# One run of probability-value products per head pair, in a two-layer hybrid trunk

## Chip, cores and metric

The kernel runs on one core of a Trainium2 chip. The metric is device time of one execution in microseconds (us). TensorE runs matmuls (PE in the profile, its weight loads PEld), VectorE is DVE, ScalarE is ACT, GpSimd is POOL, and SyncE (SP) issues most transfers.

## What is computed

Two layers over 2048 latent tokens and 256 context tokens of width 1024. Each layer norms and modulates the tokens, projects them to four head groups (a gated linear recurrence, a Fourier mix, a banded window attention, a two-dimensional neighbourhood attention), gates each group, projects back and adds to the stream. The change touches only the last step of both attentions, probabilities times values:

```python
p = jax.nn.softmax(jnp.concatenate([s_loc, s_ctx, sink_l], axis=-1), axis=-1).astype(v.dtype)
nw = 3 * SWA_BLOCK
o = (jnp.einsum('bkgnqj,bknjd->bkgnqd', p[..., :nw], v_win)
     + jnp.einsum('bkgnqc,bkcd->bkgnqd', p[..., nw:nw + CTX_LEN], vcx))
...
p = jax.nn.softmax(jnp.concatenate([s_nb, s_ctx], axis=-1), axis=-1).astype(v.dtype)
o = (jnp.einsum('bhrqkw,bhrkwd->bhrqd', p_nb, v_rows)
     + jnp.einsum('bhrqc,bhcd->bhrqd', p[..., kh * GRID_W:], vcx))
```

## The kernel before, in words

Attention works on items: one head and 128 queries. `attend` (L830) multiplies keys and queries into the one score buffer of PSUM (`pse`), DVE adds the bias and finds the row limit (L836), ACT takes the exponential (L844) into `S`. `transpose_p` turns `S` by chunks of 128 keys (L862, output `ppt`, two buffers), and the turned chunks are copied to SBUF as `pt`: the first three of a head in one copy by DVE (L872), the remaining ones in one copy by ACT (L870). For the second head of a pair it also turns the reciprocal row sums (L866) and ACT copies them (`rt`, L868). `head_out` multiplies: for each chunk `c` and each of the two heads `x` of a pair one product (L921), 128 keys by 64 value columns against 128 queries, at array position column 0 for the first head and column 64 for the second, all summed in one PSUM buffer `py`. DVE scales the result (L924). A pair has 4, 8, 10 or 12 products, and there are 136 pairs in the two layers: 1360 products, each of which the trace records as two passes. In the traced names `vd` are values of latent tokens and `vc` values of context tokens, which are the last two chunks.

`pipeline` issues the parts of neighbouring items in turn, so that the products of a pair come three items after its scores. Between these items stand the projections, `mm3` (L220 to L222, outputs `ps` of the input projections and `pso` of the output projection): three products for each 128 of 1024, on the whole 128x128 array. They are independent of the attention around them, and are called the filler below.

Nobody writes the order of an engine's queue by hand. A scheduler places the instructions of the whole program by priority (program order, unless `high_priority` raises it) and by when its model thinks that inputs and buffers are there; each engine then executes its queue in that order, and waits where something is late. Weights, activations of `prep_h` and `reload_h`, and values come by DMAs from SP.

```python
for c in range(n):
    for x, h in enumerate((r[6], r)):
        nc.tensor.matmul(py[64 * x:64 * x + 64, 0:128], h[2][c], h[5][0][c], ...)
```

`r` is the pair's second head, `r[6]` its first, `h[2]` the value chunks, `h[5][0]` the copied chunks `pt`.

Of the kernel before, what the change touches and what calls it, by code (L numbers as in the profile page):

```python
# [37 lines left out]
class Kern:  # L38
# [865 lines left out]
    def head_out(self, pool, st, i, r, stage, out):  # L904

        nc = self.nc
        S, rc, vs = r[0:3]
        if stage == 0:
            r.append(self.transpose_p(pool, S, len(vs), rc if i else None))
            if i == 0:  # L910
                st["first"] = r
            r.append(st["first"])
            return
        if i == 0:
            return
        if stage == 1:
            py = st["py"] = self.py.tile([128, 512], F32, tag="y", name="py")
            n = len(vs)
            for c in range(n):
                for x, h in enumerate((r[6], r)):  # L920
                    nc.tensor.matmul(py[64 * x:64 * x + 64, 0:128], h[2][c], h[5][0][c], start=(c == 0), stop=(c == n - 1), tile_position=(0, 64 * x))  # L921
            return
        c = out.shape[-1]
        nc.vector.tensor_tensor(out=out, in0=st["py"][:, 0:128].rearrange("p (r c) -> p r c", c=c), in1=r[5][1].rearrange("p (r c) -> p r c", c=c), op=ALU.mult)  # L924
# [457 lines left out]
```

## Time and profile before

| | |
|---|---|
| median of 3 runs | 3062.85 us (3062.26 to 3063.51) |
| the profiled execution, its own time | 3059.56 us |
| span of that execution | 3057.7 us |
| PE busy in the span | 93% (PEld 80%) |
| DVE, ACT, POOL busy | 53%, 35%, 27% |
| granted TensorE clock, mean | 0.959 |
| HBM traffic over the span | 149 GB/s |

A matmul's end in the trace is modelled, its start is recorded, so what a matmul costs in a stream of them is read from the start of one to the start of the next. A line of the timeline merges neighbours of one kind: "x3" are three passes, the time is from the first start to the last end. The last of them starts its own duration (0.27 us for `py` and `ppt`) before that end.

### The profile page before, as it was taken

The page shows a single profiled execution, that of the slowest core. Times are in us where ns is not written, and L with a number is a line of the kernel's source. Part 1 is how long each engine was busy: PE and PEld are TensorE (multiplying, and loading weights), DVE is VectorE, ACT ScalarE, POOL GpSimd, SP SyncE. Part 2 cuts the span into 40 slices and gives each one's busy share as a digit, 9 for nine tenths or more (in the row PEclk, how much of TensorE's full clock was granted, in tenths as well). Part 3 has the DMA queues.
Part 4 walks back from the last instruction along what each step waited for, and adds up shares of the span by engine and source line. Part 5 has one row for each costly group of instructions (what it writes and reads, how often), then busy time and mean ns, then how long its engine had stood idle before and what let it go on. Part 6 is the DMA issues. An engine that isn't in the chain of part 4 may idle for free. (4 is left out here: it accounts for less than half of the span.)

```text
span 3057.7 us, 56121 instructions
## 1 busy us (share of the span) xinstructions
PE 2854.0 (93%) x21206; PEld 2447.1 (80%) x21206; DVE 1618.5 (53%) x3741; ACT 1073.4 (35%) x2344; POOL 836.8 (27%) x922
## 2 busy tenths in 40 slices
PE   5989979978999999999979989999889999999998
PEld 5879879967777777777879889899778777777788
DVE  7554864475455444545654553465564546455453
ACT  3333323322343332434224323343223444343332
POOL 3242322343222111311132432333342213111132
PEclk9989979989999999999989899899999999999999
DMA  8634634254654263542554664242546643446365
GB/s 265 196 110 149 190 110 128 91 175 145 179 155 136 83 189 109 166 133 92 191 159 148 195 183 142 87 132 89 165 148 188 175 130 110 148 127 187 110 189 188
DMA packets 476684, 458.05 MB, mean 150 GB/s; under 512 B 54763, under 2 KB 355565, under 8 KB 476013
## 3 DMA queue, kind: packets, MB, share of 16 engines
q1 hardware_dynamic: 472782, 440.66, 47.2%
q0 software_dynamic: 3616, 13.64, 1.9%
q8 instruction: 173, 2.83, 0.4%
q14 instruction: 113, 0.93, 0.1%
HBM read 339.56 MB, written 114.60 MB: 149 GB/s over the span
## 5 line engine op out<-in xcount | busy, mean ns | idle before, releaser
L220 PE MATMUL ps<-whi,hh 128*128 128x256 f32 x1968 | 587.3, 298 | 33.6 <-ACT hh L258 18.2
L222 PE MATMUL ps<-whi,hl 128*128 128x256 f32 x1968 | 584.2, 297 | 9.1 <-DVE hl L259 9.1
L221 PE MATMUL ps<-wlo,hh 128*128 128x256 f32 x1968 | 583.1, 296 | 6.8 <-PEq L639 6.8
L213 POOL TENSOR_TENSOR wlo<-wraw,whi 128x512 fp32r<-128x512 f32 x208 | 284.7, 1369 | 831.3 <-ACT whi L212 801.9
L220 PEld LDWEIGHTS ps<-whi,hh 128*128 128x128 f32 x1968 | 393.0, 200 | 46.9 <-ACT hh L258 20.1
L220 PE MATMUL ps<-hh,whi 128*128 128x256 f32 x1376 | 405.6, 295 | 5.9 <-DVE nsq L376 2.6
L222 PEld LDWEIGHTS ps<-whi,hl 128*128 128x128 f32 x1968 | 391.9, 199 | 21.8 <-DVE hl L259 12.9
L221 PE MATMUL ps<-hl,whi 128*128 128x256 f32 x1376 | 405.9, 295 | 0.0
L221 PEld LDWEIGHTS ps<-wlo,hh 128*128 128x128 f32 x1968 | 393.0, 200 | 15.1 <-issue 12.8
L222 PE MATMUL ps<-hh,wlo 128*128 128x256 f32 x1376 | 404.5, 294 | 0.0
L844 ACT ACTIVATE S<-S,am 128x641 f32<-128x641 f32 (+5 forms) x272 | 226.0, 831 | 502.7 <-DVE am L836 490.3
L212 ACT CAST whi<-wraw 128x512 fp32r<-128x512 f32 x416 | 242.9, 620 | 428.1 <-DMA wraw<-w_in 193.4
L220 PE MATMUL pso<-mh,whi 128*128 128x256 f32 x1088 | 320.4, 295 | 7.3 <-DVE xo L1106 5.0
L222 PE MATMUL pso<-mh,wlo 128*128 128x256 f32 x1088 | 319.0, 294 | 3.0 <-POOL wlo L213 1.9
L221 PE MATMUL pso<-ml,whi 128*128 128x256 f32 x1088 | 318.4, 293 | 0.0
L221 PEld LDWEIGHTS ps<-hl,whi 128*128 128x128 f32 x1376 | 264.8, 192 | 35.8 <-issue 35.5
L220 PEld LDWEIGHTS ps<-hh,whi 128*128 128x128 f32 x1376 | 264.7, 192 | 32.2 <-issue 24.3
L222 PEld LDWEIGHTS ps<-hh,wlo 128*128 128x128 f32 x1376 | 264.4, 192 | 26.9 <-issue 26.5
L213 DVE TENSOR_TENSOR wlo<-wraw,whi 128x512 fp32r<-128x512 f32 x208 | 192.9, 931 | 170.4 <-ACT whi L212 162.2
L191 POOL TENSOR_TENSOR rs<-ms,mhalf 128x8 f32<-128x8 f32 (+2 forms) x140 | 172.1, 1231 | 314.6 <-DVE ms L189 305.6
L830 PE MATMUL pse<-kst,q 64*128 64x256 f32 (+2 forms) x1184 | 243.8, 457 | 3.2 <-DVE am L836 2.3
L220 PEld LDWEIGHTS pso<-mh,whi 128*128 128x128 f32 x1088 | 213.0, 196 | 25.4 <-issue 19.5
(203 smaller groups left out, 5052.8 us busy)
## 6 DMA issues: line engine op xcount, KB each, us to landing
wraw<-w_in SPq DMA_DIRECT2D x288, 256.0 KB
wraw<-w_out SPq DMA_DIRECT2D x128, 256.0 KB
adaw<-ada_w SPq DMA_DIRECT2D x82, 256.0 KB
scr_g<-ev SPq DMA_DIRECT2D x68, 256.0 KB
g<-scr_g SPq DMA_DIRECT2D x34, 512.0 KB
y<-scr_y SPq DMA_DIRECT2D x34, 512.0 KB
bias<-nbias SPq DMA_DIRECT2D x48, 256.0 KB
scr_h<-x SPq DMA_DIRECT2D x22, 512.0 KB
```

Of the source, the lines that this page charges most:

```text
L191: nc.gpsimd.tensor_tensor(out=rs, in0=ms, in1=self.mhalf.to_broadcast([128, n]), op=ALU.pow)
L212: nc.scalar.copy(hi[:, k], raw)
L213: (nc.gpsimd if i % 4 else nc.vector).tensor_tensor(out=lo[:, k], in0=raw, in1=hi[:, k], op=ALU.subtract)
L220: nc.tensor.matmul(out, ah(k), bh(k), start=(k == 0), stop=False)
L221: nc.tensor.matmul(out, ah(k), bl(k), start=False, stop=False)
L222: nc.tensor.matmul(out, al(k), bh(k), start=False, stop=(k == KB - 1))
L830: nc.tensor.matmul(p[:, lo:hi], q[r], k, start=True, stop=True, tile_position=(64 * o, 0))
L844: nc.scalar.activation(out=S[:, 0:w], in_=S[:, 0:w], func=AF.Exp, scale=-1.0, bias=m[:, 0:1], accum_out=m[:, 1:2])
```

## The change

The products of a pair are issued under the scheduler's highest priority, from the last chunk to the first, and in each chunk the second head before the first. The first product of the run then reads a chunk that is copied last.

```diff
             py = st["py"] = self.py.tile([128, 512], F32, tag="y", name="py")
             n = len(vs)
-            for c in range(n):
-                for x, h in enumerate((r[6], r)):
-                    nc.tensor.matmul(py[64 * x:64 * x + 64, 0:128], h[2][c], h[5][0][c], start=(c == 0), stop=(c == n - 1), tile_position=(0, 64 * x))
+            with self.tc.high_priority():
+                for c in range(n - 1, -1, -1):
+                    for x, h in ((1, r), (0, r[6])):
+                        nc.tensor.matmul(py[64 * x:64 * x + 64, 0:128], h[2][c], h[5][0][c], start=(c == n - 1), stop=(c == 0), tile_position=(0, 64 * x))
```

How it moves TensorE's queue is shown for one pair of twelve products in the neighbourhood attention of layer 1, where the output projection is the filler. Before, the pair's products stand in three places. The first and second, with four filler products and the turning of another head's chunks between them:

```order
L921 MATMUL py<-pt,vd 64x128
L221 MATMUL pso<-ml,whi 128x256
L222 MATMUL pso<-mh,wlo 128x256
L220 MATMUL pso<-mh,whi 128x256
L862 MATMUL ppt<-idn,S 128x128 x3
L921 MATMUL py<-pt,vd 64x128 x6
```

One product stood alone, and six followed three filler products and three transposes later. The pair's last five come behind another head's transposes, which the scores of a third head split:

```order
L862 MATMUL ppt<-idn,S 128x128
L830 MATMUL pse<-kst,q 128x384
L830 MATMUL pse<-kst,q 128x128
L830 MATMUL pse<-kst,q 128x256
L862 MATMUL ppt<-idn,S 128x128 x2
L921 MATMUL py<-pt,vd 64x128
L921 MATMUL py<-pt,vc 64x128 x4
L862 MATMUL ppt<-idn,S 128x128 x3
```

The same pair with the change, on the same engine:

```order
L220 MATMUL pso<-mh,whi 128x256
L221 MATMUL pso<-ml,whi 128x256
L922 MATMUL py<-pt,vc 64x128 x4
L922 MATMUL py<-pt,vd 64x128 x8
L862 MATMUL ppt<-idn,S 128x128 x3
L830 MATMUL pse<-kst,q 128x384
L830 MATMUL pse<-kst,q 128x128
L830 MATMUL pse<-kst,q 128x256
L862 MATMUL ppt<-idn,S 128x128 x3
```

All twelve now stand together, context chunks first, behind filler, and the transposes of each later head stand together too. Over the whole queue the 1360 products stand in 456 places before and in 136 with the change, one for each pair. (L922 is L921 of before, one line further down.)

## Rows read from the trace of the kernel before

**Rows 1.** The page's head.

```profile
span 3057.7 us, 56121 instructions
```

**Rows 2.** Busy time in the two stages of attention: stretch, length, engines, clock, DMA.

```profile
780.00:1480.00 700.00, 690.72 (x5227) 529.46 (x5226) 347.86 (x823) 269.39 (x625) 144.30 (x229) 0.99 0.46 136
2315.00:2950.00 635.00, 632.78 (x4887) 485.47 (x4886) 327.16 (x749) 256.51 (x583) 142.05 (x218) 1.00 0.52 151
```

**Rows 3.** Groups by line and shape: count, busy us, mean ns, idle before, its cause.

```profile
L921 PE MATMUL py<-pt,vd 128*64 128x128 f32 x1632 | 208.6, 293 | 4.3 <-DVE yt L924 4.3
...
L872 DVE COPY pt<-ppt 128x384 f32<-128x384 f32 x256 | 142.1, 555 | 50.3 <-PE ppt L862 46.6
...
L921 PE MATMUL py<-pt,vc 128*64 128x128 f32 x1088 | 116.5, 279 | 0.7 <-DVE pt L872 0.7
...
L870 ACT COPY pt<-ppt 128x256 f32<-128x256 f32 x176 | 65.2, 370 | 28.4 <-PE ppt L862 27.1
...
L273 DVE TENSOR_TENSOR hl<-x,hh 128x1024 fp32r<-128x1024 f32 x11 | 14.2, 1286 | 8.4 <-ACT hh L272 8.4
```

**Rows 4.** TensorE's waits, 780 to 1480 us: us in total, times, longest.

```profile
PE py L921 <- DVE pt L872: 0.7, 1, 0.7
```

**Rows 5.** TensorE's timeline, last three of a ten-product pair's four places (start, duration).

```profile
2334.99 0.29 PE L222 MATMUL ps<-hh,wlo 128*128 128x256 f32 x1
2335.21 0.43 PE L921 MATMUL py<-pt,vd 128*64 128x128 f32 x2
2335.57 0.55 PE L862 MATMUL ppt<-idn,S 128*128 128x128 f32 x3
2336.05 0.43 PE L921 MATMUL py<-pt,vd 128*64 128x128 f32 x2
2336.41 0.44 PE L862 MATMUL ppt<-idn,S 128*128 128x128 f32 x2
2336.78 0.54 PE L921 MATMUL py<-pt,vd 128*64 128x128 f32 x5
...
2337.16 0.70 PE L921 MATMUL py<-pt,vc 128*64 128x128 f32 x7
2337.80 0.39 PE L220 MATMUL ps<-hh,whi 128*128 128x256 f32 x1
2338.02 0.28 PE L221 MATMUL ps<-hl,whi 128*128 128x256 f32 x1
2338.13 0.28 PE L222 MATMUL ps<-hh,wlo 128*128 128x256 f32 x1
```

**Rows 6.** TensorE's timeline, one transpose within filler.

```profile
2400.57 0.28 PE L221 MATMUL ps<-wlo,hh 128*128 128x256 f32 x1
2400.69 0.27 PE L866 MATMUL ppt<-idn,rd 128*128 128x128 f32 x1
2400.72 0.36 PE L222 MATMUL ps<-whi,hl 128*128 128x256 f32 x1
2400.91 0.28 PE L220 MATMUL ps<-whi,hh 128*128 128x256 f32 x1
```

**Rows 7.** TensorE's timeline, scores and transposes within filler, then products.

```profile
2406.83 0.28 PE L222 MATMUL ps<-whi,hl 128*128 128x256 f32 x1
2407.04 0.93 PE L830 MATMUL pse<-kst,q 64*128 64x384 f32 x6
2407.90 0.38 PE L220 MATMUL ps<-whi,hh 128*128 128x256 f32 x1
...
2408.60 0.49 PE L862 MATMUL ppt<-idn,S 128*128 128x128 f32 x3
2409.02 0.43 PE L921 MATMUL py<-pt,vd 128*64 128x128 f32 x2
```

**Rows 8.** TensorE's timeline, a pair whose ten products stand together already.

```profile
872.48 0.88 PE L921 MATMUL py<-pt,vd 128*64 128x128 f32 x12
873.19 0.60 PE L921 MATMUL py<-pt,vc 128*64 128x128 f32 x8
```

## Prediction

> **What bounds the kernel now.** I read busy time by stage first. The page gives a span of 3057.7 us [rows 1]; the two stretches that hold attention take 700 and 635 us of it [rows 2]. [...] DVE is busy 675 us of the same 1335, ACT 526, and the DMA engines half of the time. [...] The filler is independent work that fills every hole, so in these stretches whatever TensorE no longer has to issue comes off the end.
>
> A busy TensorE is not one that multiplies at its rate, so the second view is its timeline, start to start. The reader should see there that a change of matmul shape costs. Filler to filler is 0.12 us (2338.02 to 2338.13 and so on) [rows 5]. From filler to products it is 0.22 (2334.99 to 2335.21), from products to filler 0.21, taken as 0.20, and the step behind is again 0.22 instead of 0.12 [rows 5]. Transposes start 0.11 apart: three of them last 0.49 us, the last one 0.27, so its start lies 0.22 behind the first. From 2408.60 that leaves 0.42 - 0.22 = 0.20 to the product at 2409.02 [rows 7]. Behind products the same three transposes last 0.55 [rows 5] and not 0.49 [rows 7], so their second step is 0.06 slower. A single product holds 0.16 between its two passes (0.43 - 0.27) and 0.20 more to the transposes (2335.21 to 2335.57) [rows 5].
>
> **The change, part by part.** No product, load or copy is added or removed; the order of queues changes. The priced part is TensorE's. I counted neighbours in both orders, at the level of passes, and price the difference with the steps above.
>
> *Inside the runs.* Start of the first pass to start of the last is 0.16 us for one product [rows 5], 0.81 for seven (2336.78 to 2337.16 + 0.70 - 0.27 = 2337.59) [rows 5], 1.04 for ten (872.48 to 873.19 + 0.60 - 0.27 = 873.52) [rows 8]. So each further two products add 0.22, and an odd one costs as much as a pair. Before there are 275 runs of one or two, 54 of three or four, 80 of five or six, 32 of seven or eight, 14 of nine or ten and one of eleven: 275 x 0.165 + 54 x 0.38 + 80 x 0.60 + 32 x 0.82 + 14 x 1.04 + 1.26 = 155.4 us. Now there are 8 runs of four, 8 of eight, 88 of ten and 32 of twelve (1.26, one step beyond the longest row): 3.0 + 6.6 + 91.5 + 40.3 = 141.4. Gain 14.0.
>
> *Into and out of the runs.* Transposes to products fall from 315 to 6: 309 x 0.20 = 61.8 less. Products to filler fall from 220 to 5, each with its slower next step: 215 x 0.30 = 64.5 less. Products to transposes fall from 223 to 107: 116 x 0.26 = 30.2 less. Filler to products rises from 98 to 119: 4.6 more. Products to scores rises from 7 to 24, taken like filler to scores (2406.83 to 2407.04, 0.21) [rows 7]: 3.6 more. Together 148.3 less.
>
> *What closes the gaps.* The neighbours of a vanished run now touch. Transpose to filler rises from 217 to 405; it takes 0.03 us, and the step behind it 0.19 instead of 0.12 (2400.69, 2400.72, 2400.91) [rows 6], so 188 x 0.10 = 18.8 more. Filler to filler 121 x 0.12 = 14.5 more, transpose to transpose 57 x 0.11 = 6.3 more. Filler to transpose falls by 70: 8.4 less. Filler to scores falls by 75 and transpose to scores rises by 63: 2.5 less at 0.21 each. Scores are left for transposes 135 times more and for filler and products 131 times less; I take leaving them (0.86 us from their first start to the filler) [rows 7] as equally long whatever follows, so zero. Together 28.7 more.
>
> Sum: 14.0 + 148.3 - 28.7 = 133.6 us less on TensorE, about 1 us for each of 136 pairs.
>
> *The wait that it adds.* TensorE takes its queue in order. The first product of a run waits for the pair's last copy, and behind it stand filler and the next transposes, which formerly ran while a copy was late. In the pair shown above, 17 filler products, a group of scores and three transposes stand between the last transposes it needs and its run: about 3.6 us by the steps above. The copy takes 0.37 us on ACT or 0.56 on DVE, behind at most one long instruction, as the 1.29 us subtraction of `hl` [rows 3]; that is under 2 us. So most runs should start without a wait. Nearest rows for both ends: 0.7 us for all of a stretch [rows 4], and twice the present idle time, 23 us, when everything beside TensorE is a tenth tighter. I take 8, nearer the first, since the slack is over 1.5 us.
>
> *What becomes tighter.* DVE and ACT do the same work in 134 us less: DVE rises from 51% to 56% of the two stretches (675 of 1201). `py` is held for 1 us and not for a chain of runs, which only helps the next pair. DMA traffic rises in rate by a tenth from a half-full state [rows 2]. Each at nothing; the cover is the filler, and were it gone the copies would show as TensorE's waits.
>
> [...] DVE has 675 us of work in 1335 [rows 2], which leaves it room. [...]
>
> The sum against the profiled execution: 3059.6 - 133.6 + 8 = 2934.0. The median of the runs is 3.3 above that execution, so **2937 us**.
>
> **Rivals.**
>
> 1. *The copies wait in part.* The faster queue meets copies that DVE or ACT make behind other work, and the price is half of the gain: 3063 - 67 = 2996, between 2967 and 3057. For it: half of the chunks wait for one ACT instruction behind `rt`, and an in-order TensorE has no way round. Against it: the 3.6 us of cover above.
>
> 2. *The end runs over: slower.* At each of 136 runs TensorE stops for the last copy while the filler queues behind. At 134 / 136, about 1.0 us, of wait for each run the gain is gone; at 1.5 us it is 204 - 134 = 70 us slower, 3133. The copy would have to land 4.6 us and more behind its transposes. Against it: rows 3 and 4.
>
> 3. *Nothing is gained.* Something else was the bound, and the shape changes lay in its shadow: 3063, within 6. The candidate is the emptying of PSUM by DVE and ACT. It would show as TensorE waiting for DVE or ACT, and rows 2 and 4 show hardly any. [...]
>
> That the change does not do what it says is excluded by the order: one unbroken run for each pair.
>
> **How the numbers follow.** The forecast has 0.74. Its own range comes from the unknown terms: with no new wait, and 10 us for steps read to 0.01 us of which some 1000 changed, 3063 - 144 = 2919; with 23 us of waits and no gain inside the runs, 3063 - 120 + 23 = 2966. Rival 1 has 0.14, rival 2 0.06, rival 3 0.06. I set the range at 2915 to 2985: it takes the forecast's range and the nearer part of rival 1, and leaves out the rest of it and rivals 2 and 3. A measurement of this kernel tells about 0.2% (6 us) from no change. Faster by more than that: forecast and rival 1, 0.88. Within it: rival 3, 0.06. Slower: 0.06.
>
> **What would show it.** Right: 2720 passes of products in 136 runs of 0.4 to 1.3 us; the two stretches shorter by about 70 and 63 us (72 and 64 pairs at 1 us); TensorE's idle time in them under 25 us; the clock still 1.00 there; DVE's share near 56%. Wrong: product lines with several tens of us of idle time released by `pt` copies (rivals 1 and 2), TensorE waiting for score limits or exponentials (rival 1 or 3), a second step behind a shape change that moved to the scores, or stretches that kept their length.

## The result and the profile after

The change takes 2951.29 us (median of 4 runs, 2951.03 to 2952.43) against 3063.18 us before (4 runs, 3062.26 to 3065.11): 0.9635 of the time, 95% interval 0.9618 to 0.9651. It is faster by 112 us, inside the range of 2915 to 2985 and 14 us above the predicted 2937. The same kernel, run again beside later experiments, took 2953.8.

The head of the page after, which answers to [rows 1]:

```profile
span 2949.1 us, 55777 instructions
...
PE 2718.3 (92%) x21206; PEld 2410.2 (82%) x21206; DVE 1609.3 (55%) x3741; ACT 1070.9 (36%) x2344; POOL 837.3 (28%) x922
```

The span is 108.6 us shorter, and TensorE executes the same 21206 passes. For a fair comparison I cut both traces at the first and the last score matmul of each attention. The windows view of the kernel before, cut so (stretch, length, busy time of PE, PEld, DVE, ACT and POOL, TensorE's clock, DMA share, GB/s):

```profile
772.30:1470.10 697.80, 688.52 (x5199) 527.94 (x5198) 346.58 (x821) 269.62 (x625) 142.91 (x228) 0.99 0.47 138
1470.10:2320.50 850.40, 771.22 (x5662) 723.94 (x5658) 443.69 (x986) 269.35 (x560) 274.16 (x239) 0.93 0.48 149
2320.50:2930.30 609.80, 608.40 (x4680) 463.34 (x4681) 316.77 (x731) 250.68 (x570) 135.25 (x209) 1.00 0.51 149
```

The same view of the kernel after:

```profile
772.80:1433.80 661.00, 644.68 (x5430) 537.56 (x5431) 348.81 (x834) 273.33 (x630) 150.38 (x231) 0.99 0.51 151
1433.80:2264.10 830.30, 735.70 (x5430) 687.55 (x5426) 438.67 (x972) 264.88 (x555) 270.14 (x236) 0.93 0.48 148
2264.10:2833.90 569.80, 560.90 (x4785) 461.69 (x4786) 315.65 (x740) 251.68 (x575) 139.57 (x212) 0.99 0.57 167
```

The first and third lines are the two attentions, the second is the part between them (recurrences, Fourier mix, projections). Two things stand in the attentions. They are 36.8 and 40.0 us shorter, and TensorE executes 231 and 105 more passes in them than before: filler that formerly ran outside. Counted in the trace, the filler passes inside rose by 241 and 112. At 0.12 us each [rows 5] that is 28.9 and 13.4 us of other work taken along. The middle part and the end lose exactly this filler, and become shorter by somewhat less than it is worth: the middle by 20.1 us, where 241 passes are 28.9.

The group lines by shape (count, busy us, mean ns, idle before and its cause), which answer to [rows 3]:

```profile
L862 PE MATMUL ppt<-idn,S 128*128 128x128 f32 x1360 | 243.6, 284 | 10.4 <-DVE pt L872 5.2 <-ACT pt L870 3.9 <-ACT S L844 0.7
L830 PE MATMUL pse<-kst,q 64*128 64x384 f32 x480 | 219.6, 538 | 13.6 <-DVE am L836 12.5 <-DMA kst<-scr_kd 0.8 <-issue 0.2
...
L872 DVE COPY pt<-ppt 128x384 f32<-128x384 f32 x256 | 141.3, 552 | 18.1 <-PE ppt L862 17.3
L922 PE MATMUL py<-pt,vd 128*64 128x128 f32 x1632 | 110.8, 273 | 0.0
...
L922 PE MATMUL py<-pt,vc 128*64 128x128 f32 x1088 | 89.4, 285 | 0.0
```

The products (L922) keep TensorE busy for 200.2 us instead of 325.1, with no idle time before them, 5.0 before the change. The copies are as long as they were. What is new is idle time before the scores (L830), 13.6 us, nearly all released by DVE's row limit `am`, and before the transposes (L862), 10.4 us, released by the copies that empty `ppt`. Before the change it was 3.2 and about 0.6.

TensorE's timeline after, one pair of twelve products (start, duration):

```profile
2399.77 0.66 PE L922 MATMUL py<-pt,vc 128*64 128x128 f32 x8
2400.26 1.04 PE L922 MATMUL py<-pt,vd 128*64 128x128 f32 x16
2401.23 0.55 PE L862 MATMUL ppt<-idn,S 128*128 128x128 f32 x3
2401.71 0.93 PE L830 MATMUL pse<-kst,q 64*128 64x384 f32 x6
```

First pass to last pass is 2400.26 + 1.04 - 0.27 - 2399.77 = 1.26 us, as the prediction had it one step beyond its longest row. The step to the transposes is 0.20.

Where the new waits come from is in two views of one place. DVE's timeline after:

```profile
1049.92 1.23 DVE L1083 TENSOR_TENSOR y<-y,g 128x1024 f32<-128x1024 f32 x1 [4.32 <-DMA y<-scr_y]
1051.06 0.68 DVE L213 TENSOR_TENSOR wlo<-wraw,whi 128x512 fp32r<-128x512 f32 x1
1051.66 0.28 DVE L925 TENSOR_TENSOR yt<-py,rt 128x128 f32<-128x128 f32 x1
1051.86 0.68 DVE L213 TENSOR_TENSOR wlo<-wraw,whi 128x512 fp32r<-128x512 f32 x1
1052.46 0.55 DVE L872 COPY pt<-ppt 128x384 f32<-128x384 f32 x1
```

And TensorE's at the same moment:

```profile
1050.24 0.28 PE L221 MATMUL ps<-hl,whi 128*128 128x256 f32 x1
1053.07 0.90 PE L862 MATMUL ppt<-idn,S 128*128 128x128 f32 x3 [2.55 <-DVE pt L872]
1053.62 0.56 PE L222 MATMUL ps<-hh,wlo 128*128 128x256 f32 x1
1053.98 0.41 PE L220 MATMUL ps<-hh,whi 128*128 128x256 f32 x1
1054.19 0.41 PE L221 MATMUL ps<-hl,whi 128*128 128x256 f32 x1
```

L1083 belongs to `prep_mix`: it loads the mixed heads `y` and their gates `g` for 128 tokens, DVE multiplies them (L1083), ACT rounds the product (L1084), DVE or POOL subtracts (L1085), and the output projection reads it. DVE stands 4.32 us for the load of `y`, then multiplies, then does three short things, and only then the copy that TensorE has wanted since about 1050.5. The wait of TensorE is named after `pt`, but its cause is the load. All eleven waits of over 1 us before scores and transposes in the two attentions end 0.9 to 1.9 us behind an L1083 that had itself stood for 2.3 to 5.1 us, ten of them by name for its load (for the eleventh the trace names no releaser).

### The profile page after: what moved, and what is told of

It reads as the page before. It is cut to its first block, busy times and chain, and to the rows that moved or that the text cites. A ratio compares the mean times of both kernels' runs of the same rounds, so it can differ in the third digit from the quotient of the medians.

```text
span 2949.1 us, 55777 instructions
## 1 busy us (share of the span) xinstructions
PE 2718.3 (92%) x21206; PEld 2410.2 (82%) x21206; DVE 1609.3 (55%) x3741; ACT 1070.9 (36%) x2344; POOL 837.3 (28%) x922
## 2 busy tenths in 40 slices
DMA packets 476681, 458.00 MB, mean 155 GB/s; under 512 B 54763, under 2 KB 355565, under 8 KB 476013
## 5 line engine op out<-in xcount | busy, mean ns | idle before, releaser
L830 PE MATMUL pse<-kst,q 64*128 64x256 f32 (+2 forms) x1184 | 246.6, 457 | 13.6 <-DVE am L836 12.5
L862 PE MATMUL ppt<-idn,S 128*128 128x128 f32 x1360 | 243.6, 284 | 10.4 <-DVE pt L872 5.2
```

Of the source, the lines that this page charges most:

```text
L830: nc.tensor.matmul(p[:, lo:hi], q[r], k, start=True, stop=True, tile_position=(64 * o, 0))
L862: nc.tensor.transpose(p[:, i], S[:, (c0 + i) * 128:(c0 + i + 1) * 128], self.idn)
```

## The experiments

Times are medians. The ratio to the kernel before, run beside it on the same chip, stands with its interval. Kernels that did not run side by side are better compared by their ratios than by their times: TensorE's instructions ahead of the first attention are the same ones in the same order in eleven of the fourteen traces below, and this part takes 764 to 777 us in them. The filler moves between the parts of the program, so I compare lengths by one formula. Both attentions together take 1307.6 us before, with 4514 filler passes and 11.5 us of TensorE idle. Idle time counts the gap that ends at a stretch's first score too, so it is up to 2.3 us more than length less busy time. "Gain without waits" is what an attention got shorter, plus 0.12 us for each further filler pass in it, plus its further idle time. The price applies the median start-to-start step of each kind of neighbour in the trace before, told apart by what stands ahead of it too, to every neighbour in the new queue. This finer list gives 142 us for the change, where the prediction's list by hand gave 134. A price depends on the list: one that takes each run of products whole, by its length, gives 57 us for the priority alone, 114 for the order alone and 147 for the change, so I read the column as good to some 12 us.

| kernel | runs of products | time, us | priced gain | both attentions, us | filler passes | idle, us | gain without waits |
|---|---|---|---|---|---|---|---|
| before | 456 | 3063.2 | | 1307.6 | 4514 | 11.5 | |
| the change | 136 | 2951.3 | 142 | 1230.9 | 4867 | 26.2 | 134 |
| the change again | 136 | 2953.8 | 142 | 1237.8 | 4867 | 29.7 | 130 |
| old order, priority | 289 | 3025.6 | 57 | 1294.0 | 4703 | 28.2 | 53 |
| new order, no priority | 174 | 2975.4 | 126 | 1204.6 | 4479 | 30.7 | 118 |
| third `ppt` buffer | 140 | 3007.4 | 135 | 1190.9 | 4102 | 59.7 | 115 |
| two buffers of `y` | 136 | 2970.8 | 147 | 1232.0 | 4826 | 32.5 | 134 |
| arithmetic later | 136 | 2977.0 | 145 | 1242.1 | 4841 | 33.1 | 126 |
| no loads of `y` and `g` | 137 | 2895.6 | 145 | 1203.3 | 4873 | 5.6 | 141 |
| transpose inside the run | 266 | 3037.4 | 98 | 1218.8 | 3984 | 60.3 | 74 |
| transpose beside the run | 174 | 3020.5 | 120 | 1213.2 | 4150 | 58.3 | 97 |
| `prep_mix` on POOL | 138 | 2938.5 | 144 | 1205.9 | 4725 | 19.4 | 135 |
| `y`, `g` by halves | 136 | 2929.7 | 144 | 1217.9 | 4842 | 16.1 | 134 |
| both of these | 137 | 2944.7 | 144 | 1210.0 | 4750 | 17.8 | 132 |

### The two parts of the change alone

First the priority with the old order:

```diff
             with self.tc.high_priority():
-                for c in range(n - 1, -1, -1):
-                    for x, h in ((1, r), (0, r[6])):
+                for c in range(n):
+                    for x, h in enumerate((r[6], r)):
```

> The change with the old order: chunks upwards, first head first, still at the highest priority. In its order the products stand in 289 places, 135 of them a single first product that went ahead alone. Theory A, the gain is the shape changes that TensorE no longer makes: steps priced as in the prediction fall by 57 us, new waits take 10 to 30 back, so 3016 to 3036. Rival B, the gain is that products come early by their priority: about 2951, as the change.

Measured 3025.6 us (3020.2 to 3033.8), ratio 0.9881 [0.9857, 0.9906], within the first theory's bounds.

Then the new order without the priority:

```diff
-            with self.tc.high_priority():
-                for c in range(n - 1, -1, -1):
-                    for x, h in ((1, r), (0, r[6])):
+            for c in range(n - 1, -1, -1):
+                for x, h in ((1, r), (0, r[6])):
```

> The change without the priority: last chunk first, second head first, at the normal priority. In its order the products stand in 174 places. Theory A: priced steps fall by 126 us, waits take 10 to 30 back, so 2947 to 2967. Rival B (priority): 3063, no change.

Measured 2975.4 us (2968.6 to 2978.8), ratio 0.9722 [0.9706, 0.9738]: 8 us above the upper bound expected.

The time follows how many runs the products stand in, not the priority. Reading the last-copied chunk first makes a run start only when all of it is there, which alone leaves 174 runs and gives 86 of the 112 us. Priority in the old order leaves 289 runs and gives 35. The steps hold for both queues: priced 57 and 126, found 53 and 118 without the waits. The waits are back in both, 17 and 19 us more idle in attention than before. In the old order it is also the products that wait, 9.0 us in the attentions against 0.7 in the new order; the waits of TensorE in the old-order kernel (us in total, times, longest):

```profile
PE pse L830 <- DVE am L836: 12.9, 9, 3.4
...
PE py L922 <- DVE pt L872: 8.1, 7, 2.6
```

### Is the end of a transpose buffer the wait?

A third buffer for turned chunks, taken from the PSUM bank of the norms and of the projections' own transposes:

```diff
-            p = self.pm.tile([128, 4, 128], F32, tag="m", name="ppt")
+            self.nt = getattr(self, "nt", 0) + 1
+            p = (self.ph.tile([128, 512], F32, tag="h", name="ppt").rearrange("p (a b) -> p a b", a=4) if self.nt % 3 == 0
+                 else self.pm.tile([128, 4, 128], F32, tag="m", name="ppt"))
```

> The change, with every third buffer of turned chunks taken from the PSUM bank of the norms, so that three alternate and not two. In its order 140 runs; priced steps are 7 us above the change. If TensorE's new waits for the ppt buffer (9.7 us idle from filler to transposes in the change, 0.6 before) come from there being two, they fall under 2 us and the time is 2940 to 2958. If they come from a DVE or ACT that is held up, they stay or move to the scores, and the time is 2955 to 2970.

Measured 3007.4 us (3003.6 to 3012.6), ratio 0.9825 [0.9808, 0.9842]. Outside both expectations. The idle time before transposes did not fall: it is 11.1 us, where the change has 10.4 (the part right behind filler went from 9.7 to 6.4). The bank was not free, for the program uses its one buffer elsewhere, and filler waits now for `nsq`, a step of the projections; how the one leads to the other was not traced. Waits of TensorE in the first attention of this kernel:

```profile
PE ps L220 <- DVE nsq L376: 9.3, 5, 2.7
```

The changed kernel has no such wait there. The scheduler also left 575 filler passes that the change has in the second attention to the end of the program. So this run does not decide on the buffer; it shows that borrowing this bank costs more than the wait.

### Is it the single buffer of `y`?

```diff
-            y = self.xp.tile([128, KB, 128], F32, tag="xb", name="y", bufs=1)
+            y = self.xp.tile([128, KB, 128], F32, tag="xb", name="y", bufs=2)
```

(and the same count for `sq`, which shares the buffer)

> The change, with two buffers instead of one for the loaded mixer output y of prep_mix (L1080; the squares of norm_x share them). Theory: the new waits for score limits and copies are the DVE queue standing at y times g (L1083) until the load of y has come, which had to wait for the single buffer. Then idle time of TensorE before scores and before transposes in attention falls from 22 us to under 8, DVE's waits for y in the first attention stage fall from 28.8 us to under 8, and the time is 2930 to 2942. Rival: DVE is late by its own load of work or by the transfer's speed; then 2946 to 2956 and the waits stay.

Measured 2970.8 us (2965.4 to 2980.8), ratio 0.9708 [0.9683, 0.9733]: slower than the change, and above both expectations. The theory that the load starts late because its one buffer is taken fell: SyncE issues the load 4.9 us (median) before the multiplication that waits for it, in the two traces of the change 5.3 and 4.8. The waits of DVE in this kernel:

```profile
DVE y L1083 <- DMA y<-scr_y: 74.9, 26, 8.7
```

In the change that line reads 96.5 us in 29 waits, the longest 5.5. The total is a little lower, the longest wait is longer, and idle time before scores rose from 13.6 to 22.2 us. In the first attention, where under 8 us of waits for `y` were expected, there are 31.6. The time itself says little about `y`: the second buffer of `sq` moved the instructions ahead of the first attention, where no `y` is loaded, and that part alone takes 782.3 us instead of 772.8.

### Can the arithmetic simply come later?

```diff
-            g = self.xp.tile([128, KB, 128], F32, tag="xa", name="g", bufs=3)
-            y = self.xp.tile([128, KB, 128], F32, tag="xb", name="y", bufs=1)
-            nc.sync.dma_start(y, self.y[L][s][:, :, c])
-            nc.sync.dma_start(g, self.sg[L][s][:, :, c])
+            with self.tc.high_priority():
+                g = self.xp.tile([128, KB, 128], F32, tag="xa", name="g", bufs=3)
+                y = self.xp.tile([128, KB, 128], F32, tag="xb", name="y", bufs=2)
+                nc.sync.dma_start(y, self.y[L][s][:, :, c])
+                nc.sync.dma_start(g, self.sg[L][s][:, :, c])
...
-        with self.tc.high_priority():
-            mix = {s: self.prep_mix(L, s) for s in subs}
+        mix = {s: self.prep_mix(L, s) for s in subs}
```

(and again two buffers for `sq`)

> The change, in which only the loads of prep_mix (y and g) keep the highest priority; its multiply, cast and subtraction are placed at the normal one, with two y buffers. Products in 136 runs, priced steps 3 us below the change. If the waits of scores and transposes come from DVE standing at y times g before the load has landed, placing the multiply later ends them: TensorE's idle time before scores and transposes in attention falls from 22 us to under 10 and the time is 2928 to 2945. If the DVE queue is late for another reason, or the projection itself now waits for its input, 2946 to 2975.

Measured 2977.0 us (2974.3 to 2984.6), ratio 0.9741 [0.9716, 0.9765]: a miss, a little over the rival's upper bound. Idle time before scores and transposes is 27.5 us (25.6 right behind filler), not under 10, and DVE still waits for `y`, 77.9 us in 25 waits, the longest 7.9. A lower priority, then, does not keep the multiplication from standing in DVE's order before its load is there; why the scheduler puts it there was not tested. The part ahead of the first attention takes 782.2 us here too.

### Without the loads

```diff
-            g = self.xp.tile([128, KB, 128], F32, tag="xa", name="g", bufs=3)
             y = self.xp.tile([128, KB, 128], F32, tag="xb", name="y", bufs=1)
-            nc.sync.dma_start(y, self.y[L][s][:, :, c])
-            nc.sync.dma_start(g, self.sg[L][s][:, :, c])
-            nc.vector.tensor_tensor(out=y, in0=y, in1=g, op=ALU.mult)
+            one = self.idn.rearrange("p (o c) -> p o c", o=1).to_broadcast([128, KB, 128])
+            nc.vector.tensor_tensor(out=y, in0=one, in1=one, op=ALU.mult)
```

> The change without the loads of y and g in prep_mix: the multiply takes the identity matrix twice, so the gating of the mixed heads is left out, and 34 MB less are read. Products in 137 runs, priced steps 3 us below the change. If waiting for these loads on DVE and ACT is what makes scores and transposes wait, TensorE's idle time before them falls from 22 us to under 6 and the time is 2915 to 2935 (with the end of each layer a little shorter too). If not, 2940 to 2951.

This kernel leaves out the loads of the mixed heads and gates; the three operations behind them run on the identity matrix. Measured 2895.6 us (2890.1 to 2898.3), ratio 0.948 [0.9457, 0.9504], 19 us below the lowest time expected. That is 56 us below the change by the times, and 47 by the ratios. Its waits before scores and transposes:

```profile
PE pse L830 <- DMA kst<-scr_kd: 1.5, 1, 1.5
...
PE ppt L862 <- ACT S L844: 1.2, 1, 1.2
PE pse L830 <- DVE am L836: 1.0, 2, 0.8
```

Idle time in the attentions falls to 5.6 us, where the change has 26.2 and the kernel before 11.5. DVE does the same arithmetic (busy 669 us in the attentions, 664 in the change), so its amount of work is not the cause of these waits, the loads are. At most 11.5 - 5.6 = 5.9 us of it could have been there before, so at least 14.7 of the 20.6 us that go here are what the change added. It also moves 36 MB less (422 instead of 458), and the middle part loses 15 to 20 us of idle time as well; how much of this the changed kernel could get back while it still loads, this run does not say.

### The price of a broken run

A transpose of a chunk already copied, whose result nobody reads, in the middle of each run. It goes to the bank of the norms and of the projections' own transposes, so "unused" in the two expectations is not right:

```diff
                 for c in range(n - 1, -1, -1):
+                    if c == n // 2 - 1:
+                        nc.tensor.transpose(self.ph.tile([128, 512], F32, tag="h", name="dm")[:, 0:128], r[5][0][n - 1], self.idn)
                     for x, h in ((1, r), (0, r[6])):
```

> The change with one more transpose for each pair, of a copied chunk into an unused PSUM bank, in the middle of its run of products, which it breaks in 105 of 136 cases (266 runs in all). Theory A: it adds 136 transposes and two shape changes each; priced steps are 44 us above the change, so 2985 to 3008. If shape changes cost nothing and only the work counts, 136 times 0.11 us: 2966.

And the same work behind the second head's transposes, where it breaks no run itself (the scheduler leaves 174 runs all the same):

```diff
             if rc is not None and c0 + w == n:
+                nc.tensor.transpose(self.ph.tile([128, 512], F32, tag="h", name="dm")[:, 0:128], S[:, (n - 1) * 128:n * 128], self.idn)
+            if rc is not None and c0 + w == n:
                 rd = pool.tile([128, 2, 64], F32, tag="rd", name="rd", bufs=2)
```

> The change with the same number of added transposes, into the same unused bank, but behind the transposes of the pair's second head; the scheduler then leaves 174 runs. Theory A: priced steps are 22 us above the change, so 2963 to 2986, and 15 to 30 us below the kernel with the transpose in the run. If shape changes cost nothing, the two are equal.

Measured 3037.4 us (3029.4 to 3047.2), ratio 0.9944 [0.9921, 0.9967], and 3020.5 us (3012.4 to 3029.8), ratio 0.9882 [0.9845, 0.9918]. Both times are above what was expected; the difference, 17 us (the ranges overlap by a microsecond), is within it. It was meant to be what the place alone costs, priced 22; but filler and waits fall otherwise in the two kernels as well, and without them the difference is 23. TensorE's timeline of the first kernel shows one such break:

```profile
902.03 0.39 PE L924 MATMUL py<-pt,vd 128*64 128x128 f32 x4
902.35 0.33 PE L922 MATMUL dm<-idn,pt 128*128 128x128 f32 x1
902.61 0.88 PE L924 MATMUL py<-pt,vd 128*64 128x128 f32 x12
```

From the last pass before the break (902.03 + 0.39 - 0.27 = 902.15) to the first behind it are 0.46 us: 0.20 in and 0.26 out. The two kernels are 86 and 69 us slower than the change for one small transpose a pair. Like the third buffer they use the projections' bank, and like it they show filler waiting for `nsq` in the first attention (8.7 and 8.4 us) and leave over 500 filler passes of the second attention to the end. That they share this, while the other kernels wait there for 0.5 us at most, is shown; why the scheduler then fills the second attention less was not settled.

### The change again, and two ways to take DVE off the load

The unchanged kernel, as a base on the same chip:

> The change itself, unaltered, beside the next two kernels on the same chip: 2945 to 2957 if the chips of the later runs are like that of the first measurement. If it comes out at 2965 or more, the 15 to 30 us by which the earlier experiments lay above their estimates belong to the chip and not to the edits.

Measured 2953.8 us (2945.5 to 2964.9), ratio 0.9653 [0.9617, 0.969]. As expected.

The arithmetic of `prep_mix` on POOL alone, with POOL's small copy for the reciprocals given to DVE:

```diff
-                nc.gpsimd.tensor_copy(out=rd, in_=rc...)
+                nc.vector.tensor_copy(out=rd, in_=rc...)
...
-            nc.vector.tensor_tensor(out=y, in0=y, in1=g, op=ALU.mult)
-            nc.scalar.copy(hh[:, :, c], y)
-            (nc.gpsimd if t else nc.vector).tensor_tensor(out=hl[:, :, c], in0=y, in1=hh[:, :, c], op=ALU.subtract)
+            nc.gpsimd.tensor_tensor(out=y, in0=y, in1=g, op=ALU.mult)
+            nc.gpsimd.tensor_copy(out=hh[:, :, c], in_=y)
+            nc.gpsimd.tensor_tensor(out=hl[:, :, c], in0=y, in1=hh[:, :, c], op=ALU.subtract)
```

> The change with prep_mix's multiply, cast and subtraction all on POOL, and the copy of reciprocal sums (rd) that stood on POOL on DVE instead: nothing that scores or copied chunks wait for is queued behind the loads of y and g any more. Products in 138 runs, priced steps 2 us below the change. If DVE and ACT standing for those loads is the cause, TensorE's idle time before scores and transposes falls from 22 us to under 8 and the time is 15 to 25 us below the change on the same chip; if filler now waits for its slower input, the gain is lost again in waits of the output projection.

Measured 2938.5 us (2937.2 to 2945.9), ratio 0.9605 [0.9578, 0.9631], 15 us below the change on the same chip, at the near end of what was expected (the ranges of the two touch, and the intervals of their ratios overlap). The waits of POOL in this kernel:

```profile
POOL y L1083 <- DMA y<-scr_y: 123.9, 24, 8.9
```

The load is as late as ever, but it holds up an engine that the attention hardly needs. Idle time in the attentions falls from 29.7 to 19.4 us; before scores and transposes 13.3 are left of 26.8 (4.9 right behind filler, which is what the expectation counts).

`y` and `g` laid out in memory by halves of 128 tokens, so that a load takes 4 KB pieces instead of eight of 512 B; some stores become shorter, 512 B instead of 1 KB:

```diff
-            nc.sync.dma_start(y, self.y[L][s][:, :, c])
-            nc.sync.dma_start(g, self.sg[L][s][:, :, c])
+            nc.sync.dma_start(y, self.y[L][s][t])
+            nc.sync.dma_start(g, self.sg[L][s][t])
...
-        self.sg[L], self.y[L] = sc("g", [128, KB, SUB]), sc("y", [128, KB, SUB])
+        self.sg[L], self.y[L] = sc("g", [2, 128, KB, 128]), sc("y", [2, 128, KB, 128])
```

(the stores of `y` and `g` follow the new layout)

> The change with the scratch of mixed heads and of gates laid out by halves of 128 tokens, so that prep_mix loads 4 KB for each partition in one piece and not eight of 512 B. If the transfer's own duration is what DVE stands for, its waits for y fall from 28.8 us in the first attention stage to under 15 and the time is 8 to 20 us below the change on the same chip; if the transfers wait in the queue instead, it is within 5 us.

Measured 2929.7 us (2923.2 to 2933.9), ratio 0.9564 [0.9536, 0.9592], 24 us below the change on the same chip, a little more than the theory expected, and the best of the kernels that compute everything. The theory's other sign failed: DVE's waits for `y` in the first attention are 25.0 us, where under 15 was expected. Over the whole kernel (L1084 is L1083 of the change, one line further down):

```profile
DVE y L1084 <- DMA y<-scr_y: 70.5, 30, 4.4
```

And the transfers on its page:

```profile
DMA packets 442697, 458.01 MB, mean 156 GB/s; under 512 B 55851, under 2 KB 321581, under 8 KB 442029
```

The repeated change has 96.1 us in 31 waits, the longest 5.9, and 476681 packets for the same bytes. TensorE's idle time in the attentions falls from 29.7 to 16.1 us. Packets of 512 B take 29 ns on average in the repeated change and packets of 4 KB 211 ns here, so 17.5 and 19.4 GB/s for one DMA engine, about a tenth apart. SyncE also issues a load of `y` in 0.33 us instead of 0.54 (medians), and a load that DVE stands for is there 4.1 us behind the start of its issue instead of 4.8. So the loads come sooner, but most of the 24 us is not accounted for by that, and how much is due to the stores that changed too, or to where filler fell, was not separated.

Both together:

> The change, with the arithmetic of prep_mix on POOL and the y and g scratch laid out by halves of 128 tokens, both at once; the products stand in 137 runs. Theory (the loads of y and g, and what stands behind them on DVE and ACT, are the loss): the change had 12.2 us of idle of TensorE before scores and 11.9 before transposes in its repeated run; POOL alone left 8.2 and 2.3, the layout alone 5.8 and 6.5, the kernel without the loads 2.4 and 0. Together about 2 to 5 us are left before scores and under 3 before transposes, and the time is 2910 to 2930, below either alone (2938.5 and 2929.7). Rival (the two runs were faster by where the filler fell, not by the loads: their filler counts in attention differ too): the two do not add, and the time is 2930 to 2950.

Measured 2944.7 us (2940.5 to 2948.6, 5 runs), ratio 0.963 [0.961, 0.9649]. The theory's time failed and the rival's holds. By its ratio this kernel is no faster than the change (0.9635 and 0.9653), although the two parts alone came out lower (0.9605 and 0.9564). The theory's idle times came about before scores, 2.9 us, but not quite before transposes, 4.1. TensorE's waits in this kernel:

```profile
PE pso L220 <- POOL mh L1085: 4.8, 1, 4.8
...
PE ppt L863 <- ACT S L845: 2.7, 1, 2.7
PE pse L831 <- DVE am L837: 2.6, 5, 1.0
```

Idle time in the attentions is 17.8 us, no less than with the layout alone, because 7 us of it now stand before filler. Of these 4.8 are one wait of the output projection for its own input, which POOL now rounds: the loss that the run with `prep_mix` on POOL alone had named as its rival. And the middle part, with its filler priced as above, is 5.8 us longer than in the repeated change, where the layout alone had made it 6.7 shorter. What lengthens the middle was not settled; POOL, which has `prep_mix` there as well, is busy for 298 us of it instead of 271. So the two gains are not shown to be gains on the loads alone: the rival, that they came from where the filler fell, is not excluded. That the loads cause the waits in the attentions rests on the kernel without them, and on the eleven places above.

## Why the prediction was right, and 14 us off

**The step from one matmul shape to another: right.** The mechanism and its sum held. Without the waits the attentions gained 133.8 us by the formula above, the prediction 133.6 (the repeated run gives 130, so the match to a microsecond is luck; and the terms for the runs before add up to 156.0 as they are written, not 155.4, so its sum should read 134.1). By kinds of neighbours, start to start over the whole trace: inside the runs 14.5 less (14.0 predicted, 14.5 by its own terms), transposes to products 63.4 less (61.8), products to filler 43.7 less (215 x 0.20 = 43.0 without the slower step behind), products to transposes 24.0 less (30.2). The best evidence is the table: in all nine queues that leave the projections' bank alone, with the products in 136 to 289 runs, the gain without waits is 87 to 98% of the price by the finer list (85 to 104% by the list that takes each run whole). The three with the borrowed bank reach 76 to 85%; why they fall short was not settled.

**The chip's own limit: not the copies' rate.** DVE is busy 664 of 1231 us in the two attentions, 54%, where 56% was predicted. The candidate of rival 3, the emptying of PSUM, did not decide here: products waited for copies for 0.2 us in all. The transposes did wait for copies to empty their buffer, 9.1 us, behind the loads.

**The wait: the term that was mis-sized, and its place was wrong.** The prediction put 8 us of new waits at the first product of a run, "for the pair's last copy". There they are 0.2 us. The slack of several microseconds that it read was right. The idle time rose at the scores and the transposes instead: in the attentions from 11.5 to 26.2 us, so 14.7. After its filler is priced, the middle part is 8.7 us longer than it should be, and the remaining parts 1.7. Together 14.7 + 8.7 + 1.7 = 25.1, and 133.8 - 25.1 = 108.7, the difference of the spans but for rounding. Each of these terms is a difference of lengths, so that they add up proves nothing.

The step that failed is "What becomes tighter ... each at nothing; the cover is the filler". In the attentions the runs showed in its place that a late load holds TensorE up through DVE: 20.6 us of idle time go when the loads go. The loads were late before the change, too, and the trace of the kernel before has it. Its waits of DVE over the whole span, and one place in the timelines of DVE and TensorE:

```profile
DVE y L1082 <- DMA y<-scr_y: 70.6, 25, 6.2
...
1095.44 1.23 DVE L1082 TENSOR_TENSOR y<-y,g 128x1024 f32<-128x1024 f32 x1 [3.01 <-DMA y<-scr_y]
1096.59 0.28 DVE L924 TENSOR_TENSOR yt<-py,rt 128x128 f32<-128x128 f32 x1
...
1096.93 0.69 PE L921 MATMUL py<-pt,vd 128*64 128x128 f32 x2 [2.94 <-DVE yt L924]
```

The 4.3 us that [rows 3] books to `yt` are two waits, 2.94 and 1.40 us, and both end 0.26 us behind such a multiplication that had stood still. The prediction did not follow that row to its cause. In the two attentions DVE stands 47.6 us ahead of 23 such multiplications before, and 78.9 ahead of 25 after.

What lengthens the middle part is open. Its idle time (length less busy) rose from 79.2 to 94.6 us, 88.7 in the repeated run, and it has 241 filler passes less. But missing filler is not enough as a reason: the new order without priority has as many filler passes there as the kernel before, 4486 and 4485, and 90.0 us of idle time, while the kernel without the loads has 215 fewer, and 74.2.

**The idle time predicted in attention:** "under 25 us" was just missed, 26.2 (25.2 as length less busy). By [rows 2] it was 1335 - 690.7 - 632.8 = 11.5 before, and the 23 us of waits at the far end of the forecast are twice that.

**The clock, the places, the lengths.** 136 runs of 0.4 to 1.3 us: right. Clock 1.00 in both: 0.99. Stretches shorter by 70 and 63: as lengths no, 36.8 and 40.0, since filler moved in, which the prediction had left where it was. With that filler counted they are 36.8 + 28.9 = 65.7 and 40.0 + 13.4 = 53.4, and 72.9 and 60.9 when the waits are added.

**The rivals.** Half of the gain was not lost (rival 1), TensorE did not stop at each run (rival 2), and the kernel gained (rival 3). Rival 1 had the right idea of who would be late, DVE and ACT, and the wrong reason: not their own long instructions but the loads that they stand for.

## What to carry to other kernels

Read what the step between two matmul shapes costs from start to start, count the neighbours in the old and in the new queue, and multiply; here that gave the gain, apart from waits, to within 15% in nine queues. Then ask which instruction in an in-order queue waits for a transfer, and what stands behind it: the wait shows under the name of the innocent copy behind it, as TensorE's 2.55 us for `pt` here, behind DVE's 4.32 us for `y`. A small one in the trace before is worth following to its cause: here it had grown after the change. If filler moves between stages, count it before you compare their lengths.

## What the runs showed of the hardware that was not expected

A wait of TensorE here cost more than its idle time. The windows view of the change around the wait shown above:

```profile
1040.00:1050.40 10.40, 8.78 (x74) 6.95 (x72) 5.14 (x10) 5.31 (x11) 1.57 (x2) 1.00 0.61 178
...
1053.00:1054.00 1.00, 0.93 (x5) 0.94 (x6) 1.00 (x4) 0.00 (x0) 1.00 (x1) 0.50 0.96 291
1054.00:1055.00 1.00, 1.00 (x6) 1.00 (x6) 0.41 (x2) 0.50 (x1) 0.77 (x1) 0.50 1.08 346
...
1056.00:1058.00 2.00, 2.00 (x14) 1.46 (x14) 0.91 (x3) 1.15 (x4) 0.69 (x2) 1.00 1.03 362
```

After 2.55 us of idle time the granted clock stands at 0.50, and the filler steps take 0.21 us (1053.98 to 1054.19) instead of 0.12; from 1056 on it is 1.00 again. By these steps some 3 us of work at 0.50 are an estimated 3 x (1 - 0.12 / 0.21) = 1.3 us more, on top of the 2.55. The change's other two waits of over 2 us in the attentions, 2.68 and 2.35 us in the second, are followed by the same fall (0.50 from 2626.0 to 2629.4, 0.51 from 2783.0 to 2786.4). Not every wait is: behind one of 1.88 us in the first attention the clock stands at 1.00 (1378.3 to 1390.0), and in the repeated run one of 2.39 us was followed by no fall. In the kernel before, the stretch behind the wait of 2.94 us shown above is all at 0.50:

```profile
1098.00:1106.00 8.00, 8.00 (x38) 4.96 (x36) 4.64 (x9) 5.78 (x13) 1.27 (x1) 0.50 0.90 276
```
